# Two transformer blocks on one core: the tiles that TensorE reads are moved to multiples of 512 bytes

## The chip, the cores and the metric

The kernel runs on one NeuronCore of a Trainium2 chip, as one launch. The metric is the device time of an execution in microseconds (us), from which the median of several runs is taken. The engines are named as in the profile: PE is TensorE's matmul, PEld its weight load, DVE is VectorE, ACT is ScalarE, POOL is GpSimd, SP issues DMAs.

## The reference

The input x has 256 tokens of 1,024 features. Two models run one after the other, all in float32:

```python
for i in range(2):                                   # first model, two layers
    x = x + mixer_i(rms_norm(x, norm_mix[i]))        # layer 0: NSA (8 heads) and differential attention (4 heads)
                                                     # layer 1: MoBA attention, 16 heads
    x = x + square(relu(rms_norm(x, norm_mlp[i]) @ mlp_w1[i])) @ mlp_w2[i]      # 1024 -> 4096 -> 1024
x = rms_norm(x, norm_final)
                                                     # second model, one layer
proj = rms_norm(x) @ w_in                            # xa, ga, q, k, v, f, g_a, g_b
y_a = gelu(ga) * rg_lru(conv(xa));  y_b = forgetting_attention(q, k, v, f)
x = x + rms_norm((sigmoid(g_a) * (y_a @ w_proj_a) + sigmoid(g_b) * (y_b @ w_proj_b)) @ w_out)
gate, val = split(conv(rms_norm(x) @ w_up))          # 1024 -> 2 * 3072
x = x + rms_norm((gelu(gate) * val) @ w_down)        # 3072 -> 1024
```

## The kernel before

Activations lie transposed in SBUF, features on the 128 partitions and the 256 tokens along a partition. `x` is the residual stream, 8 feature tiles of 256 tokens. Every projection is computed in the type `float32r` with both operands split in two: a high part and the rest, `a = ah + al`. A product then takes three matmuls: `wh*xh`, `wh*xl`, `wl*xh`.

Weights stream from DRAM. `w_load` fetches a chunk of 1 MB into one of three `raw` buffers by a DMA on SP's queue; `w_parts` splits half a chunk (a unit of 1,024 columns) into `whi` by ACT (L233) and `wlo` by DVE (L234). There are six buffers of 4,096 bytes per partition for each of the two, and `w_next` keeps three units ahead of the one that is used.

Where TensorE multiplies:

- `mm3` (L275, L276, L277): the weights are loaded as the stationary operand, 128 columns, and 256 columns of the activation move through. The activation is `gg_`, the split input of a projection (`gh` and `gl` are its two halves), or `oh` and `ol`, the split output of an attention (tiles `oh`/`ol` of layer 0, `oh1`/`ol1`, `oh2`/`ol2`). `gen_pair` uses it for the projections from the residual stream, `gen_half` for those from an attention.
- `mm2` (L281, L282), in `gen_deep`, for the second matrix of an MLP: 512 columns move in L281 (both halves of `hh`, `hh2` or `yh`), 256 in L282.
- `gen_nat` (L457 to L459) and `gen_wide` (L479 to L481) the other way round: the activation `gg_` is stationary and 256 or 512 columns of `whi` or `wlo` move.

```python
    def mm3(o, wh, wl, xh, xl, start, stop, skip=False):
        nc.tensor.matmul(out=o, lhsT=wh, rhs=xh, start=start, stop=False, skip_group_check=skip)
        nc.tensor.matmul(out=o, lhsT=wh, rhs=xl, start=False, stop=False, skip_group_check=skip)
        nc.tensor.matmul(out=o, lhsT=wl, rhs=xh, start=False, stop=stop, skip_group_check=skip)
```

The order of all work is written out by hand. `weave` interleaves a chain of projection steps with the steps of an attention (`maps_gen`) or of the recurrence (`rg_gen`); elsewhere `run` takes the steps of one projection one after another. The time line of a run: layer 0's projections and attention to 156 us, its MLP to 338, layer 1's attention to 454 and MLP to 636, the second model's mixer to 943, its up projection with convolution and gelu (`evac_up`) to 1085, its down projection to 1157, the end.

Where a tile lies in SBUF follows from the order of the pools and, within a pool, from the order in which its tiles are first asked for; each is rounded up to 32 bytes, and a pool that is closed gives its place to the next. Its place is the same in all 128 partitions. The first bytes in the kernel before, and what is left of them after division by 512:

| tile | first byte | mod 512 |
|---|---|---|
| `vec`, `cs`, `ones` (pool `cp`) | 16512, 18624, 21728 | 128, 192, 224 |
| `x`, `gg_` (pool `xp`) | 22912, 31104 | 384 |
| `acc`, `sq` (pool `np`) | 47488, 51712 | 384, 0 |
| `raw` (three) | 54848 ... | 64 |
| `whi` (six), `wlo` (six) (pool `wp`) | 80192 ..., 104768 ... | 320 |
| `hh` of the first MLP, of the second | 146752, 129344 | 320 |
| `hh2`, `yh` | 129344 | 320 |
| `qT` of layer 0 (pool `a0`) | 146752 | 320 |
| `kcT` of layer 0 | 173824 | 256 |
| `wcmp`, and later in the same place `oh`, `ol` of layer 0 | 176032, 184224 | 416 |
| `oh1`, `ol1`, `oh2`, `ol2` | 155968, 164160, 167232, 175424 | 320 |

Slices of these tiles that TensorE reads begin at multiples of 512 bytes from the tile's first byte, so that a tile's remainder is that of all its reads: `gg_` has 2,048 bytes for a feature tile (1,024 each for the high and the low part), a weight tile 512 bytes for a feature tile and 128 columns.

Of the kernel before, what the change touches and what calls it, by code (L numbers as in the profile page):

```python
# [7 lines left out]
F32 = mybir.dt.float32  # L8
# [61 lines left out]
def kernel(  # L70
# [29 lines left out]
    cp = ctx.enter_context(tc.tile_pool(name="cp", bufs=1))  # L100
    xp = ctx.enter_context(tc.tile_pool(name="xp", bufs=1))
    np_ = ctx.enter_context(tc.tile_pool(name="np", bufs=2))
    rawp = ctx.enter_context(tc.tile_pool(name="rawp", bufs=3))
    wp = ctx.enter_context(tc.tile_pool(name="wp", bufs=6))
    dp = ctx.enter_context(tc.tile_pool(name="dp", bufs=1, space=DRAM))
# [6 lines left out]
    cs = cp.tile([128, NCST], F32, name="cs")  # L112
    ones = cp.tile([128, 128], F32, name="ones")
    mhalf = cp.tile([128, 8], F32, name="mhalf")
    x = xp.tile([128, KT, T], F32, name="x")
    gg_ = xp.tile([128, KT, 2, T], FR, name="gg_")
    g_ = Halves(gg_)
# [4 lines left out]
    def V(n, i=None, m=1):  # L122
        o, w = VEC[n]
        if i is None:
            return vec[:, o:o + w]
        return vec[:, o + i:o + i + m]
# [10 lines left out]
    def add_stream(ap, units, n=None, small=False):  # L137
        for i in range(ap.shape[0] if n is None else n):
            chunks.append((ap[i], units, small))
# [43 lines left out]
    add_stream(w_up, U8)  # L183
    add_stream(w_dn, U8)

    W = Ctl()
    W.raw = []
    W.q = []
    W.ci = 0
    W.ui = 0  # L190
    NT = (7, 11)

    def w_load():
        ci = len(W.raw)
        if ci >= len(chunks):
            return
        ap, units, small = chunks[ci]
        n = sum(a * b for a, b in units)
        if small:
            t = rawp.tile([128, n], F32, tag="raws", name="raws", bufs=1)  # L200
        else:
            t = rawp.tile([128, 2048], F32, tag="raw", name="raw")
        if ci == 0:
            W.part = lambda a, b: nc.sync.dma_start(out=t[:, a:b], in_=ap[:, a:b])
        else:
            nc.sync.dma_start(out=t[:, :n], in_=ap)
        W.raw.append(t)
# [525 lines left out]
    nc.sync.dma_start(out=cs, in_=cst)  # L733
    nc.sync.dma_start(out=vec[:, 72:], in_=vecs[:, 72:])
    w_load()
    tb_t = cp.tile([33, 16], F32, name="tb_t")
    nc.vector.memset(tb_t[32:33, :], NEGB)
    nc.vector.memset(ones, 1.0)
    nc.vector.memset(mhalf, -0.5)
    warm = cp.tile([128, 8], F32, name="warm")  # L740
    nc.scalar.activation(out=warm, in_=mhalf, func=AF.Square)

    wps = pst.tile([128, 512], F32, tag="t", name="wps")
# [78 lines left out]

    A0 = ExitStack()
    ap0 = A0.enter_context(tc.tile_pool(name="a0", bufs=1))
    qT = ap0.tile([128, 4, T], F32, name="qT")
    ksT = ap0.tile([128, T], F32, name="ksT")
    kwT = ap0.tile([128, T], F32, name="kwT")
# [11 lines left out]
    kcT = ap0.tile([128, 2, 16], F32, name="kcT")  # L839
    vcb = ap0.tile([128, 8, 64], F32, name="vcb")  # L840
    nlam = ap0.tile([128, 1], F32, name="nlam")
    wcmp = [ap0.tile([128, 2048], F32, tag="e8", name="wcmp%d" % i, bufs=2) for i in range(2)]
    for i in range(2):
        nc.sync.dma_start(out=wcmp[i], in_=w_cmp[i])

# [289 lines left out]
    nc.vector.tensor_tensor(out=sqs[2], in0=sqs[2], in1=sqs[3], op=ALU.add)  # L1135
    norm.parts = [sqs[k][:, a, :] for k in (0, 2) for a in range(2)]
    norm.tail = 3
    sgain = cp.tile([128, 1], F32, name="sgain")
    have = {}

    def note(n, f):
# [79 lines left out]
    def log1pe(pool, z, n, pre):  # L1221

        e = pool.tile([128, n], F32, name=pre + "e")
        d = pool.tile([128, n], F32, name=pre + "d")
        q = pool.tile([128, n], F32, name=pre + "q")

        def s0():
            nc.vector.scalar_tensor_tensor(out=e, in0=z, scalar=-1.0, in1=z, op0=ALU.mult, op1=ALU.min)
            nc.scalar.activation(out=e, in_=e, func=AF.Exp)

        def s1():
            nc.vector.tensor_scalar(out=d, in0=e, scalar1=2.0, scalar2=None, op0=ALU.add)
            nc.vector.reciprocal(out=d, in_=d)
            nc.vector.tensor_tensor(out=e, in0=e, in1=d, op=ALU.mult)

        def s2():
            nc.vector.tensor_tensor(out=d, in0=e, in1=e, op=ALU.mult)
            nc.vector.tensor_scalar(out=q, in0=d, scalar1=1.0 / 19.0, scalar2=None, op0=ALU.mult)

        def poly(cs_):  # L1240
            for c in cs_:
                nc.vector.scalar_tensor_tensor(out=q, in0=q, scalar=1.0 / c, in1=d, op0=ALU.add, op1=ALU.mult)

        def s7():
            nc.vector.scalar_tensor_tensor(out=q, in0=q, scalar=1.0, in1=e, op0=ALU.add, op1=ALU.mult)
            nc.vector.tensor_scalar(out=q, in0=q, scalar1=2.0, scalar2=None, op0=ALU.mult)

        steps = [s0, s1, s2] + [lambda c=c: poly(c) for c in ((17, 15), (13, 11), (9, 7), (5, 3))] + [s7]
        return steps, q
# [63 lines left out]
        ],  # L1313
        gen_half(0, 4, oh, ol, residual_add, ready=lambda: len(hdone) >= 2),
    )
    nsp = cp.tile([128, 10], F32, name="nsp")
    psp = cp.tile([128, 10], F32, name="psp")
    hb = cp.tile([128, 20], F32, name="hb")
    hm = cp.tile([128, 16], F32, name="hm")
    sp_steps, sp_q = log1pe(cp, V("lam"), 10, "sp")  # L1320

    def sp_fin():
# [15 lines left out]
    bias_ctx.close()  # L1338


    gc = cp.tile([128, 8], F32, name="gc")
    nc.vector.tensor_tensor(out=gc, in0=V("fin"), in1=V("pre2"), op=ALU.mult)
    nA, nB = Norm(), Norm()
    mlp(norm, lambda j: gc[:, j:j + 1], nA, nB)
# [642 lines left out]
```

## Time and profile before

| | |
|---|---|
| median of 3 runs | 1167.9 us (1167.79 to 1168.95) |
| the profiled execution | 1170.1 us, of which 1168.3 us are its span (first to last instruction) |
| granted TensorE clock, mean of the span | 0.987 of full speed |
| PE busy | 1133.2 us, 97% of the span, 8,367 matmuls |
| DVE busy, ACT busy, POOL busy | 69%, 54%, 16% |

A matmul's busy time in the profile overlaps that of the next (a matmul of 256 columns is listed with some 280 ns, and one starts every 113 to 120 ns), so the pace of a stream is read from the starts of its matmuls, and PE's share of busy time only says that it hardly ever stands still.

### The profile page before, as it was taken

To read this page: it belongs to the slowest core of one execution; us is meant where nothing else is said; L and a number is where in the kernel's file an instruction comes from. 1 tells how busy PE (TensorE), PEld (TensorE's weight loads), DVE (VectorE), ACT (ScalarE), POOL (GpSimd) and SP (SyncE) were. 2 spreads that over 40 slices of the span, in tenths; PEclk is the share of its full clock that TensorE was granted. 3 is DMA by queue.
4 is the path that set the end of the run, shared out by engine and by line. 5 is a ranking of instruction groups with operands and counts; after the bars stand their busy time and mean duration, and the time that the engine had idled before them with its cause. 6 is when DMAs were issued, how large, how long until landed. Compare 5 with 4: busy or idle time off the path is not lost.

```text
span 1168.3 us, 20796 instructions
## 1 busy us (share of the span) xinstructions
PE 1133.2 (97%) x8367; PEld 1036.7 (89%) x8367; DVE 806.9 (69%) x1436; ACT 630.7 (54%) x1120; POOL 187.6 (16%) x228
## 2 busy tenths in 40 slices
PE   8999999999999999999999999999999999999996
PEld 7987799998889889999889896899799999999885
DVE  5767766665545776576455787866677589999843
ACT  4446556553434555556444677645464656666642
POOL 2014320000010123000001000032310123222211
PEclk8999999999999999999999999999999989999998
DMA  8841244555454333455455453564455425455641
GB/s 324 291 143 73 74 181 145 201 197 203 158 216 180 116 131 145 151 185 206 188 213 207 152 197 123 173 228 149 158 181 206 175 89 167 163 177 180 208 153 37
DMA packets 31297, 199.90 MB, mean 171 GB/s; under 512 B 3594, under 2 KB 6042, under 8 KB 9056
## 3 DMA queue, kind: packets, MB, share of 16 engines
q1 hardware_dynamic: 28832, 187.23, 44.4%
q0 software_dynamic: 2080, 11.08, 2.9%
q8 instruction: 66, 1.08, 0.4%
q14 instruction: 31, 0.25, 0.1%
q10 hardware_dynamic: 288, 0.26, 0.1%
HBM read 197.43 MB, written 3.22 MB: 172 GB/s over the span
## 4 chain that ended last, share of the span: by engine, by line
PE 77%; DVE 14%; ACT 3%; issue 2%; POOL 2%; DMA 1%; SPq 0%; POOLq 0%; ACTq 0%
PE g L281 15%; PE g L275 14%; PE g L277 13%; PE g L276 13%; PE g L282 7%; DVE y L1693 4%; DVE wlo L234 4%; PE rgp L1462 2%; PE pt L664 1%; PE g L479 1%; PE g L481 1%; PE g L480 1%; PE o L714 1%; ACT whi L233 1%; DVE u L1681 1%
## 5 line engine op out<-in xcount | busy, mean ns | idle before, releaser
L234 DVE TENSOR_TENSOR wlo<-raw,whi 128x1024 fp32r<-128x1024 f32 (+2 forms) x356 | 421.0, 1213 | 107.6 <-ACT whi L233 107.4
L275 PE MATMUL g<-gg__91,whi 128*128 128x256 f32 x1632 | 463.1, 284 | 4.0 <-ACT whi L233 2.4
L277 PE MATMUL g<-gg__91,wlo 128*128 128x256 f32 x1632 | 459.7, 282 | 4.1 <-DVE wlo L234 4.1
L276 PE MATMUL g<-gg__91,whi 128*128 128x256 f32 x1632 | 457.4, 280 | 0.5 <-DVE gg__91 L270 0.4
L233 ACT CAST whi<-raw 128x1024 fp32r<-128x1024 f32 (+2 forms) x356 | 350.2, 1024 | 15.5 <-PE g L276 7.8
L275 PEld LDWEIGHTS g<-gg__91,whi 128*128 128x128 f32 x1632 | 308.5, 189 | 11.5 <-issue 5.4
L277 PEld LDWEIGHTS g<-gg__91,wlo 128*128 128x128 f32 x1632 | 308.4, 189 | 8.3 <-DVE wlo L234 8.2
L276 PEld LDWEIGHTS g<-gg__91,whi 128*128 128x128 f32 x1632 | 308.9, 189 | 1.2 <-DVE gg__91 L270 0.7
L281 PE MATMUL g<-hh,whi 128*128 128x512 f32 x704 | 247.4, 397 | 1.4 <-DVE u L1681 1.4
L282 PE MATMUL g<-hh,wlo 128*128 128x256 f32 x704 | 196.8, 280 | 0.2 <-DVE wlo L234 0.2
L281 PEld LDWEIGHTS g<-hh,whi 128*128 128x128 f32 x704 | 132.2, 188 | 33.6 <-ACT q L1702 1.7
L282 PEld LDWEIGHTS g<-hh,wlo 128*128 128x128 f32 x704 | 132.6, 188 | 0.5 <-DVE wlo L234 0.5
L339 POOL TENSOR_TENSOR acc<-acc,sq 128x256 f32<-128x256 f32 x53 | 42.3, 805 | 463.8 <-ACT sq L335 462.8
L653 POOL TENSOR_TENSOR p<-p,rr 128x384 f32<-128x384 f32 x56 | 49.1, 877 | 210.6 <-DVE rr L648 80.1
L638 ACT ACTIVATE p<-p,nm 128x256 f32<-128x256 f32 x112 | 49.9, 449 | 45.2 <-DVE nm L629 45.0
L1693 DVE SCALAR_TENSOR_TENSOR y<-u,cw,y 128x255 f32<-128x255 f32 (+1 forms) x96 | 60.2, 687 | 0.0
L275 PE MATMUL g<-oh,whi 128*128 128x256 f32 x192 | 55.6, 290 | 0.0
L277 PE MATMUL g<-oh,wlo 128*128 128x256 f32 x192 | 54.3, 283 | 0.0
L1208 ACT ACTIVATE u<-u 128x512 f32<-128x512 f32 x32 | 20.2, 632 | 62.8 <-DVE u L1207 62.8
L276 PE MATMUL g<-ol,whi 128*128 128x256 f32 x192 | 54.1, 282 | 0.0
L750 DVE TENSOR_TENSOR x<-x,g 128x256 f32<-128x256 f32 x32 | 13.5, 421 | 56.7 <-PE g L282 56.2
L267 DVE TENSOR_TENSOR hh<-u,hh 128x512 fp32r<-128x512 f32 x32 | 22.2, 693 | 43.2 <-ACT hh L266 43.2
(325 smaller groups left out, 1340.7 us busy)
## 6 DMA issues: line engine op xcount, KB each, us to landing
raw<-in_w_in_dram SPq DMA_DIRECT2D x30, 1024.0 KB, 4.9
raw<-in_w_up_dram SPq DMA_DIRECT2D x24, 1024.0 KB, 4.9
raw<-in_w_m1a_dram SPq DMA_DIRECT2D x16, 1024.0 KB, 4.8
raw<-in_w_m2a_dram SPq DMA_DIRECT2D x16, 1024.0 KB, 4.9
raw<-in_w_m1b_dram SPq DMA_DIRECT2D x16, 1024.0 KB, 4.8
raw<-in_w_m2b_dram SPq DMA_DIRECT2D x16, 1024.0 KB, 4.9
raw<-in_w_od_dram SPq DMA_DIRECT2D x12, 1024.0 KB, 4.9
raw<-in_w_dn_dram SPq DMA_DIRECT2D x12, 1024.0 KB, 4.8
```

Of the source, the lines that this page charges most:

```text
L233: nc.scalar.copy(out=hi[:, a:b], in_=t[:, off + a:off + b])
L234: nc.vector.tensor_tensor(out=lo[:, a:b], in0=t[:, off + a:off + b], in1=hi[:, a:b].bitcast(F32), op=ALU.subtract)
L275: nc.tensor.matmul(out=o, lhsT=wh, rhs=xh, start=start, stop=False, skip_group_check=skip)
L276: nc.tensor.matmul(out=o, lhsT=wh, rhs=xl, start=False, stop=False, skip_group_check=skip)
L277: nc.tensor.matmul(out=o, lhsT=wl, rhs=xh, start=False, stop=stop, skip_group_check=skip)
L281: nc.tensor.matmul(out=ps.rearrange("p a t -> p (a t)"), lhsT=wh, rhs=X.both(k), start=start, stop=False, skip_group_check=True)
L282: nc.tensor.matmul(out=ps[:, 0, :], lhsT=wl, rhs=X.h[:, k, :], start=False, stop=stop, skip_group_check=True)
L339: nc.gpsimd.tensor_tensor(out=self.acc, in0=self.acc, in1=dst, op=ALU.add)
L638: nc.scalar.activation(out=p[:, c0:c1], in_=p[:, c0:c1], func=AF.Exp, scale=-1.0, bias=nm[:, b:b + 1], accum_out=sm[:, b:b + 1],)
L653: nc.gpsimd.tensor_tensor(out=pv, in0=pv, in1=w, op=ALU.mult)
L1462: nc.tensor.matmul(out=ps[c, m, :], lhsT=w[:, m, prs[pi], c], rhs=xc[:, half * 5 + pi, :], start=n == 0, stop=n == len(nb), skip_group_che ...
L1693: nc.vector.scalar_tensor_tensor(out=y[:, a, d:], in0=u[:, a, 0:T - d], scalar=cw[:, w, c:c + 1], in1=y[:, a, d:], op0=ALU.mult, op1=ALU.add)
```

## The change

No instruction is added, removed or reordered. Two tiles that nothing writes or reads (`pad`) are put in, of 128 bytes per partition ahead of `x` and of 64 ahead of the weight buffers; the small tiles of pool `cp` are asked for at its start; and in layer 0's pool `wcmp` is asked for first and no longer after `nlam`.

```diff
+    def pad(pool, n):
+        pool.tile([128, n], F32, tag="pad", name="pad", bufs=1)
+
     rawp = ctx.enter_context(tc.tile_pool(name="rawp", bufs=3))
     wp = ctx.enter_context(tc.tile_pool(name="wp", bufs=6))
...
     mhalf = cp.tile([128, 8], F32, name="mhalf")
+    tb_t = cp.tile([33, 16], F32, name="tb_t")
+    warm = cp.tile([128, 8], F32, name="warm")
...
+    gc = cp.tile([128, 8], F32, name="gc")
+    pad(xp, 32)
     x = xp.tile([128, KT, T], F32, name="x")
     gg_ = xp.tile([128, KT, 2, T], FR, name="gg_")
...
+    pad(wp, 16)
     W = Ctl()
...
     ap0 = A0.enter_context(tc.tile_pool(name="a0", bufs=1))
+    wcmp = [ap0.tile([128, 2048], F32, tag="e8", name="wcmp%d" % i, bufs=2) for i in range(2)]
     qT = ap0.tile([128, 4, T], F32, name="qT")
...
     nlam = ap0.tile([128, 1], F32, name="nlam")
-    wcmp = [ap0.tile([128, 2048], F32, tag="e8", name="wcmp%d" % i, bufs=2) for i in range(2)]
```

## Rows read from the trace of the kernel before

**Rows 1.** The page's first lines: span; busy time, share and instructions by engine.
```profile
span 1168.3 us, 20796 instructions
PE 1133.2 (97%) x8367; PEld 1036.7 (89%) x8367; DVE 806.9 (69%) x1436; ACT 630.7 (54%) x1120; POOL 187.6 (16%) x228
```

**Rows 2.** The chain of work that ended last, shares by engine.
```profile
PE 77%; DVE 14%; ACT 3%; issue 2%; POOL 2%; DMA 1%; SPq 0%; POOLq 0%; ACTq 0%
```

**Rows 3.** Stretches: length, busy PE, PEld, DVE, ACT, POOL; clock; DMA share; GB/s.
```profile
184.00:248.00 64.00, 64.00 (x546) 64.00 (x545) 44.34 (x49) 37.84 (x48) 0.00 (x0) 1.00 0.56 198
649.00:710.00 61.00, 61.00 (x461) 50.97 (x462) 54.66 (x102) 42.49 (x72) 0.90 (x4) 1.00 0.41 151
943.00:1085.00 142.00, 138.25 (x1138) 134.59 (x1137) 137.91 (x211) 96.48 (x162) 39.74 (x47) 1.00 0.48 163
```

**Rows 4.** PE's waits, of the list the one for split weights: us, times, longest.
```profile
PE g L277 <- DVE wlo L234: 4.1, 19, 0.4
```

**Rows 5.** The costliest groups of the page: busy us, mean ns; idle before.
```profile
L234 DVE TENSOR_TENSOR wlo<-raw,whi 128x1024 fp32r<-128x1024 f32 (+2 forms) x356 | 421.0, 1213 | 107.6 <-ACT whi L233 107.4
L275 PE MATMUL g<-gg__91,whi 128*128 128x256 f32 x1632 | 463.1, 284 | 4.0 <-ACT whi L233 2.4
L281 PE MATMUL g<-hh,whi 128*128 128x512 f32 x704 | 247.4, 397 | 1.4 <-DVE u L1681 1.4
```

**Rows 6.** Timeline of PE, start and length: two streams on `gg_`, first and last.
```profile
183.61 0.28 PE L275 MATMUL g<-gg__91,whi 128*128 128x256 f32 x1
...
247.91 0.28 PE L275 MATMUL g<-gg__91,whi 128*128 128x256 f32 x1
...
679.44 0.28 PE L276 MATMUL g<-gg__91,whi 128*128 128x256 f32 x1
...
702.22 0.28 PE L276 MATMUL g<-gg__91,whi 128*128 128x256 f32 x1
```

**Rows 7.** Timeline of PE: two streams on attention outputs, first matmul and next stream's first.
```profile
145.49 0.29 PE L275 MATMUL g<-oh,whi 128*128 128x256 f32 x1
...
156.29 0.28 PE L275 MATMUL g<-gg__91,whi 128*128 128x256 f32 x1
...
885.27 0.28 PE L275 MATMUL g<-oh,whi 128*128 128x256 f32 x1
...
908.30 0.28 PE L275 MATMUL g<-gg__91,whi 128*128 128x256 f32 x1
```

**Rows 8.** Timeline of PE: second matrix of the first MLP, then of the second.
```profile
248.27 0.39 PE L281 MATMUL g<-hh,whi 128*128 128x512 f32 x1
...
338.01 0.40 PE L281 MATMUL g<-hh,whi 128*128 128x512 f32 x1
...
546.89 0.39 PE L281 MATMUL g<-hh,whi 128*128 128x512 f32 x1
...
635.64 0.28 PE L275 MATMUL g<-gg__91,whi 128*128 128x256 f32 x1
```

**Rows 9.** Timeline of PE: part of a stream with moving weights.
```profile
71.31 0.28 PE L459 MATMUL g<-whi,gg__91 128*128 128x256 f32 x1
...
73.70 0.28 PE L459 MATMUL g<-whi,gg__91 128*128 128x256 f32 x1
```

**Rows 10.** Timeline of PE: sums of squares, one moving column, 128 stationary ones.
```profile
19.07 1.05 PE L346 MATMUL nsum<-ones,qT 128*128 128x1 f32 x8
19.98 1.03 PE L346 MATMUL nsum<-ones,kvd 128*128 128x1 f32 x8
20.88 0.28 PE L275 MATMUL gs<-gg__91,whi 128*24 128x256 f32 x1
...
932.06 1.05 PE L346 MATMUL nsum<-ones,sq 128*128 128x1 f32 x8 [0.53 <-ACT sq L335]
```

**Rows 11.** Timeline of PE: a projection to 16 columns, so 16 stationary columns.
```profile
711.07 0.28 PE L276 MATMUL gs<-gg__91,whi 128*16 128x256 f32 x1
...
712.66 0.39 PE L479 MATMUL g<-whi,gg__91 128*128 128x512 f32 x1
```

More of the change, by code (lines that the diff above doesn't have):

```diff
@@ L114 @@
     mhalf = cp.tile([128, 8], F32, name="mhalf")
+    tb_t = cp.tile([33, 16], F32, name="tb_t")
+    warm = cp.tile([128, 8], F32, name="warm")
+    sgain = cp.tile([128, 1], F32, name="sgain")
+    nsp = cp.tile([128, 10], F32, name="nsp")
+    psp = cp.tile([128, 10], F32, name="psp")
+    hb = cp.tile([128, 20], F32, name="hb")
+    hm = cp.tile([128, 16], F32, name="hm")
+    gc = cp.tile([128, 8], F32, name="gc")
+    pad(xp, 32)
     x = xp.tile([128, KT, T], F32, name="x")
@@ L735 @@
     w_load()
-    tb_t = cp.tile([33, 16], F32, name="tb_t")
     nc.vector.memset(tb_t[32:33, :], NEGB)
@@ L739 @@
     nc.vector.memset(mhalf, -0.5)
-    warm = cp.tile([128, 8], F32, name="warm")
     nc.scalar.activation(out=warm, in_=mhalf, func=AF.Square)
@@ L1137 @@
     norm.tail = 3
-    sgain = cp.tile([128, 1], F32, name="sgain")
     have = {}
@@ L1315 @@
     )
[L1316 to L1319, printed above, removed]
     sp_steps, sp_q = log1pe(cp, V("lam"), 10, "sp")
@@ L1338 @@
     bias_ctx.close()
-    gc = cp.tile([128, 8], F32, name="gc")
     nc.vector.tensor_tensor(out=gc, in0=V("fin"), in1=V("pre2"), op=ALU.mult)
```

## The prediction

> **What bounds the kernel now.** I read the page's engine table first: PE is busy 97% of the span, and no other engine over 69% [rows 1]. The chain of waits says the same from the other side: 77% of the chain that ended last is PE work, 14% DVE [rows 2]. Next the stretches. In a plain projection, 184 to 248 us, PE fills all of its time while DVE works 44 of 64 us; from 943 to 1085 us, the up projection, DVE works 137.9 of 142 us, so there PE follows DVE and a faster PE wins nothing [rows 3]. PE's waits are short: the late half of the split weights costs 4.1 us in 19 waits over the whole run [rows 4]. So outside the up projection the time is the number of matmuls times the pace at which PE starts them.
>
> That pace is the place to look, because a change of addresses can act on nothing else. The groups give 284 ns for a matmul of 256 columns [rows 5], but they overlap; the timeline gives starts. On `gg_` from 183.61 to 247.91 us there are 546 steps: 117.8 ns each. From 679.44 to 702.22 us, same line, same tiles, 201 steps: 113.3 ns [rows 6]. On `oh` of layer 0 90 steps take 10.80 us, on `oh2` 192 steps take 23.03 us: 120.0 ns in both [rows 7]. In the second matrix of the first MLP 254 pairs (L281 and L282, 512 and 256 columns) take 89.74 us, 353.3 ns a pair; in the second MLP 256 pairs take 88.75 us, 346.7 ns [rows 8]. The clock was at full speed, 2.4 GHz (granted 1.00), in all the stretches of [rows 3], and if a column takes a cycle, which I assume, 256 are 106.7 ns, so 6.6 to 13.3 ns of every matmul are stall.
>
> Two things are to be seen. First, identical tiles run at two paces: a stream keeps one of them for a long time and can change it only after an interruption. That is a phase between PE's two SBUF reads, the moving operand of one matmul and the weights of the next. Second, the worst pace belongs to addresses. Moving tile and weights lie at (384, 320) mod 512 for `gg_`: 117.8 or 113.3. They lie at (320, 320) for `oh2` and (416, 320) for layer 0's `oh`: 120.0. With the roles exchanged, weights moving at 320 and `gg_` stationary at 384, 21 steps take 2.39 us, 113.8 ns [rows 9].
>
> **The change part by part.** The tiles of `cp` that are asked for earlier were already in `cp`; their sum is unchanged and `x` would still begin at 22912 = 44 x 512 + 384. The pad of 128 bytes takes it and `gg_` to 0. Everything behind moves by 128, `whi` and `wlo` to 448, and the pad of 64 takes these to 0. From there all pools lie 192 bytes further, and 320 + 192 = 512: `hh`, `hh2`, `yh`, `oh1`, `ol1`, `oh2`, `ol2` reach 0. Layer 0's `oh` and `ol` take the place of `wcmp`, now first in its pool: 0. So all pairs become (0, 0), which no row of before has.
>
> The instructions are the same in the same order on every engine and queue; SP and POOL issue the same DMAs. The pads are never written. One reuse moves: with `wcmp` first, the early part of the first MLP's `hh` lies where `oh` and `ol` were. Their last reader ends before 156.6 us, and PE has left them for `gg_` at 156.29 [rows 7]; nothing can be written to `hh` before the MLP's own first products, later on the same engine. No wait, cost 0.
>
> What remains is the pace at (0, 0). The bounds from the rows: if only one of the two reads is at work, alignment shows nothing. Weight loads alone (one moving column) take 1.05 us for eight at 320 and 1.05 us for eight at 0, and the eight from 19.98 to 20.88 us are 112 ns apart [rows 10]. Moving reads nearly alone, with weights of 16 columns, at 384: 14 steps in 1.59 us, 113.6 ns [rows 11]. So the stall above 113 ns is a conflict of the two reads. 320 is an odd multiple of 64, 384 is a multiple of 128. Count the operands off 128: none has been seen; one gives 117.8 or 113.3, whichever side it is on; two give 120.0, for 416 as for 320, though their distances differ (96 and 0). [...] With none off, I take the better pace that the trace shows for the same work.
>
> The sum, outside the first 25 us and the up projection, over gaps that no wait interrupts, by the timeline's starts:
> - L275 to L277 on `gg_`: of 4,896, some 3,720 (1,127 in the up projection and 48 in the start win nothing), mean 117.0 ns over 3,611 steps (676 are already at 113.3). To 113.3: 3.65 x 3,611 = 13.1 us.
> - the same on the attention outputs: 555 steps at a mean of 119.8, 6.5 ns each: 3.6 us.
> - second MLP matrices and `yh`: about 770 pairs at a mean of 350.9 to 346.7: 3.2 us. Two thirds are at 353.3 now, a third at 346.7 [rows 8].
> - `gen_nat` and `gen_wide`: 135 and 186 steps, 0.7 us together.
>
> In all 20.6 us. Against the profiled execution that is 1170.1 - 20.6 = 1149.5; this execution lies 2.2 us above the median of the runs, so the median goes from 1167.9 to 1147.3. The cover: ACT and DVE must split weights some 3% faster. A unit of 24 matmuls lasts 24 x 113.3 = 2.72 us, a split of `wlo` 1.21 us [rows 5], and in the stretch at 113.3 ns, where the recurrence runs too, DVE was at 54.7 of 61 us and PE still full [rows 3]. If DVE falls behind there, nothing is lost, since that stretch is at the target already. Bounds: below, all pairs down to the weight loads' 112 ns, about 34 us by the same counts (5.0 x 3,611, 7.8 x 555, and 12.3 x 770 with a pair at 2 x 113.3 + 112 = 338.6, 1.7 for the rest); above, 120.0 everywhere (next part).
>
> **The rivals.**
> - *Equal remainders collide more.* The trace's only pairs with the same remainder in all their steps are (320, 320), and `oh2` is never at anything but 120.0 once settled [rows 7]. After the change all pairs are equal. If distance decides and not the multiple of 128, `gg_` goes from 117.0 to 120.0: 3.0 x 3,611 = 11.0 us, 0.7 for the small streams: 1167.9 + 11.7 = 1179.6. It decides as soon as the mean on `gg_` is over 117.0 plus what the other tiles give. Against: (416, 320) is as bad at another distance, and `hh` at (320, 320) does have a better state [rows 8].
> - *Addresses decide nothing, phase does.* The Trainium skill, page "SBUF — State Buffer", section "Who interferes with whom", gives PE two independent read ports and says that it waits on no one; alignment would then win nothing, 1167.9. Apart from the page: if a stream keeps the phase of its last restart and restarts fall as before, it is 1167.9. If all streams fell into the slow one, 676 steps x 4.45 and 256 pairs x 6.6 would be lost, 4.7 us, and 1.1 us won where 120.0 falls to 117.8: 1171.5. Against it stand 120.0 on two sets of attention tiles and 117.8 or 113.3 on `gg_` with the same loop [rows 6, 7].
> - *Aligned reads are better than anything seen.* Weight loads set the pace: 1167.9 - 34 = about 1134.
>
> **How the numbers follow.** Forecast, alignment frees the stalls to the better pace or part of the way to it (1140 to 1158): 0.45. Beyond that, down to the loads' pace: 0.10. Addresses decide nothing, or gains and losses cancel: 0.15, most of it within 0.2%, which is 2.3 us and about what a measurement of this kernel can tell from no change. Equal remainders collide, or the slow phase wins: 0.30, 1171 to 1181. I predict 1147.3. A range from 1136 to 1180 leaves out some 0.05 at the lower end and 0.1 at the upper; the forecast's own range is 1140 to 1158. Faster 0.55, same 0.13, slower 0.32.
>
> **What would show it.** Right: the timeline on `gg_` outside the up projection at 113.3 ns or less from start to start in nearly all streams, `oh` and `oh2` as fast as `gg_`, the first MLP's pairs at 346.7 or less, granted clock, weight split and DMA rows unchanged, and the up projection still 142 us long. Wrong: 120.0 on `gg_` (the first rival), the same mixture of 113.3 and 117.8 with `oh` still apart (the second), or PE at a better pace but waiting for `wlo` by as much as it wins, which would move the bound to DVE.

## The result: slower by 0.9%

| | before | after |
|---|---|---|
| median of three runs | 1167.9 us | 1179.0 us (1177.84 to 1179.56) |
| ratio to before, 95% interval | | 1.0091, 1.0068 to 1.0114 |
| profiled execution, its span | 1170.1 us, 1168.3 us | 1177.84 us, 1176.1 us |
| mean pace of L288 to L290 on `gg_`, outside the up projection | 117.0 ns | 119.9 ns |

I had predicted 1147.3 us and faster; the range, to 1180, holds the result, but at the end of the first rival, "equal remainders collide more", which gave 1179.6.

The changed kernel's lines stand 13 further down than before in the helpers, so L275 to L277 are now L288 to L290, L281 and L282 are L294 and L295, L233 and L234 are L246 and L247. First the page's opening lines and the chain's shares by engine, which answer to [rows 1, 2]:

```profile
span 1176.1 us, 20795 instructions
PE 1144.4 (97%) x8367; PEld 1049.9 (89%) x8367; DVE 808.6 (69%) x1436; ACT 630.1 (54%) x1120; POOL 187.7 (16%) x228
PE 78%; DVE 14%; ACT 3%; issue 2%; POOL 2%; DMA 1%; SPq 0%; POOLq 0%; ACTq 0%; DVEq 0%
```

PE is busy 11.2 us longer with the same 8,367 matmuls; DVE, ACT and POOL are within 1.7 us of before. Nothing was added and nothing waits more: PE itself is slower. The costliest groups say how (busy us, mean ns of one, then idle time before them and what ended most of it):

```profile
L247 DVE TENSOR_TENSOR wlo<-raw,whi 128x1024 fp32r<-128x1024 f32 (+2 forms) x356 | 421.6, 1214 | 107.0 <-ACT whi L246 106.8
L288 PE MATMUL g<-gg__100,whi 128*128 128x256 f32 x1632 | 469.6, 288 | 4.0 <-ACT whi L246 2.5
L290 PE MATMUL g<-gg__100,wlo 128*128 128x256 f32 x1632 | 465.6, 285 | 1.4 <-DVE wlo L247 0.2
L294 PE MATMUL g<-hh,whi 128*128 128x512 f32 x704 | 248.0, 398 | 1.4 <-DVE u L1686 1.4
```

L288's mean rises from 284 to 288 ns [rows 5], while the split of the weights keeps its 1.21 us and PE's wait for `wlo` falls from 4.1 us [rows 4] to 0.2. The stretches of [rows 3], same columns:

```profile
184.00:248.00 64.00, 64.00 (x536) 64.00 (x535) 43.35 (x49) 37.12 (x48) 0.00 (x0) 1.00 0.56 198
943.00:1085.00 142.00, 138.03 (x1094) 134.30 (x1095) 136.27 (x214) 94.73 (x163) 39.87 (x48) 0.98 0.45 155
```

In the plain projection, with the clock at full speed in both, 536 matmuls fit where 546 did. The second stretch now takes in the head of the up projection, whose first matmul starts at 946.20 us where it started at 937.28: up to 951.4 us PE's granted clock is 0.50 there (1.2 GHz), as it was up to 943.7 before, hence the 0.98. By the starts of its matmuls the up projection lasts 147.4 us before and 147.5 now. The timeline of PE gives the pace (start, length):

```profile
183.72 0.28 PE L288 MATMUL g<-gg__100,whi 128*128 128x256 f32 x1
...
250.32 0.40 PE L294 MATMUL g<-hh,whi 128*128 128x512 f32 x1
...
340.77 0.40 PE L492 MATMUL g<-whi,gg__100 128*128 128x512 f32 x1
...
550.50 0.40 PE L294 MATMUL g<-hh,whi 128*128 128x512 f32 x1
...
640.95 0.28 PE L288 MATMUL g<-gg__100,whi 128*128 128x256 f32 x1
...
689.80 0.28 PE L288 MATMUL g<-gg__100,whi 128*128 128x256 f32 x1
...
710.20 0.28 PE L290 MATMUL g<-gg__100,wlo 128*128 128x256 f32 x1
...
894.28 0.28 PE L288 MATMUL g<-oh,whi 128*128 128x256 f32 x1
...
917.32 0.28 PE L288 MATMUL g<-gg__100,whi 128*128 128x256 f32 x1
```

From 183.72 to 250.32 us there are 555 steps: 120.0 ns each, where [rows 6] had 117.8. From 689.80 to 710.20 there are 170: again 120.0, where [rows 6] had 113.3 in the same projection. No stream on `gg_` keeps a faster pace. `oh2`, 192 steps from 894.28 to 917.32, is at 120.0 as in [rows 7]. The second matrices of the two MLPs (256 pairs from 250.32, 256 from 550.50) are at 353.3 ns a pair each; in [rows 8] the second had 346.7.

The balance, by starts: 3,611 x 2.9 = 10.5 us more on `gg_`; the second MLP 256 x 6.7 = 1.7 more; `gen_nat`, now at 120.0, 0.6 more; the 186 wide steps fell from 233.2 to 228.2, 0.9 less; the last projection's pairs (`hh2`) fell from 353.4 to 346.7 in their long stretch, some 1.0 less. Together 10.9. The medians differ by 11.1, the two profiled executions by 7.8 only: the one of the kernel before lies 2.2 us above its median, that of the changed kernel 1.2 below. By the starts, these 3 us lie in the first 25 us and in steps that a wait or another operation interrupts.

### The profile page after: what moved, and what is told of

Read it like the earlier page. It is cut to its first block, busy times and chain, and to the rows that moved or that the text cites. A ratio compares the mean times of both kernels' runs of the same rounds, so it can differ in the third digit from the quotient of the medians.

```text
span 1176.1 us, 20795 instructions
## 1 busy us (share of the span) xinstructions
PE 1144.4 (97%) x8367; PEld 1049.9 (89%) x8367; DVE 808.6 (69%) x1436; ACT 630.1 (54%) x1120; POOL 187.7 (16%) x228
## 4 chain that ended last, share of the span: by engine, by line
PE 78%; DVE 14%; ACT 3%; issue 2%; POOL 2%; DMA 1%; SPq 0%; POOLq 0%; ACTq 0%; DVEq 0%
PE g L294 15%; PE g L288 14%; PE g L289 14%; PE g L290 14%; PE g L295 7%; DVE y L1698 4%; DVE wlo L247 4%; PE rgp L1467 2%; PE pt L677 1%; PE g L492 1%; PE o L727 1%; PE g L494 1%; PE g L493 1%; DVE u L1686 1%; PE s L633 1%
## 5 line engine op out<-in xcount | busy, mean ns | idle before, releaser
L247 DVE TENSOR_TENSOR wlo<-raw,whi 128x1024 fp32r<-128x1024 f32 (+2 forms) x356 | 421.6, 1214 | 107.0 <-ACT whi L246 106.8
L288 PE MATMUL g<-gg__100,whi 128*128 128x256 f32 x1632 | 469.6, 288 | 4.0 <-ACT whi L246 2.5
L290 PE MATMUL g<-gg__100,wlo 128*128 128x256 f32 x1632 | 465.6, 285 | 1.4 <-DVE wlo L247 0.2
L289 PE MATMUL g<-gg__100,whi 128*128 128x256 f32 x1632 | 464.1, 284 | 0.5 <-DVE gg__100 L283 0.4
L246 ACT CAST whi<-raw 128x1024 fp32r<-128x1024 f32 (+2 forms) x356 | 349.7, 1022 | 16.2 <-PE g L289 7.9
L288 PEld LDWEIGHTS g<-gg__100,whi 128*128 128x128 f32 x1632 | 315.0, 193 | 11.4 <-issue 5.5
L290 PEld LDWEIGHTS g<-gg__100,wlo 128*128 128x128 f32 x1632 | 314.8, 193 | 5.1 <-DVE wlo L247 5.1
L289 PEld LDWEIGHTS g<-gg__100,whi 128*128 128x128 f32 x1632 | 315.0, 193 | 1.2 <-DVE gg__100 L283 0.7
L294 PE MATMUL g<-hh,whi 128*128 128x512 f32 x704 | 248.0, 398 | 1.4 <-DVE u L1686 1.4
L295 PE MATMUL g<-hh,wlo 128*128 128x256 f32 x704 | 197.2, 280 | 0.1
L294 PEld LDWEIGHTS g<-hh,whi 128*128 128x128 f32 x704 | 132.2, 188 | 33.8 <-ACT q L1707 1.7
L295 PEld LDWEIGHTS g<-hh,wlo 128*128 128x128 f32 x704 | 132.8, 189 | 0.4 <-DVE wlo L247 0.4
L288 PE MATMUL g<-oh,whi 128*128 128x256 f32 x192 | 55.6, 290 | 0.0
L290 PE MATMUL g<-oh,wlo 128*128 128x256 f32 x192 | 54.3, 283 | 0.0
```

The source lines that it names most:

```text
L246: nc.scalar.copy(out=hi[:, a:b], in_=t[:, off + a:off + b])
L247: nc.vector.tensor_tensor(out=lo[:, a:b], in0=t[:, off + a:off + b], in1=hi[:, a:b].bitcast(F32), op=ALU.subtract)
L294: nc.tensor.matmul(out=ps.rearrange("p a t -> p (a t)"), lhsT=wh, rhs=X.both(k), start=start, stop=False, skip_group_check=True)
L295: nc.tensor.matmul(out=ps[:, 0, :], lhsT=wl, rhs=X.h[:, k, :], start=False, stop=stop, skip_group_check=True)
```

## The experiments

Two theories stood after the result. *Distance*: what counts is how far the first byte of the moving tile and that of the stationary tile lie from each other modulo some power of two, and distance 0 is bad. *Place*: what counts is where each of them lies against a boundary, and the multiple of 512 itself is bad. The expectations name a third, *restart*: any shift deals the two paces anew.

### The streams by themselves

A program with nothing but matmuls on tiles begun at chosen bytes. "Pair" below is the three-product stream of L288 to L290 (ns a matmul), "deep" the pairs of L294 and L295 (ns for both), "wide" 512 moving columns. Each was begun three times, after interruptions of different length.

```
CASES = [(d, 0) for d in (0, 16, 32, 48, 64, 80, 96, 112, 128, 192, 256, 384)] + [
    (64, 64), (32, 32), (0, 64), (0, 32), (0, 96)]   # (moving, stationary)
```

> Not the two blocks: matmul streams alone, on two tiles whose places are chosen (moving at m, weights at w bytes past a multiple of 512), each pair with the loops of mm3, of mm2 and with 512 moving columns, restarted three times; the output is not the blocks' one. If the distance of the two reads decides, and with a period of 128 bytes: at (0,0), (128,0), (256,0), (384,0), (64,64) and (32,32) the mm3 stream runs at 120.0 ns a matmul; at (64,0), (192,0) and (0,64) at 117.8 or 113.3, by the restart. If the place of each tile by itself decides: (64,64) and (32,32) differ from (0,0), and (128,0) from (256,0). If neither, all pairs show the same mixture. For 16, 32, 48, 80, 96, 112 no theory has a number; one below 113.3 would be the place to put the tiles.

Measured, first byte of the moving and of the stationary tile past a multiple of 512:

| moving, stationary | pair | deep | wide |
|---|---|---|---|
| 0, 0 | 120.0 119.9 119.9 | 346.4 346.4 353.0 | 226.6 to 228.6 |
| 64, 64 | 119.8 120.0 119.9 | 353.5 | 227.7 |
| 32, 32 | 119.8 | 346.6 346.6 353.9 | 227 |
| 256, 0 | as 0, 0 | as 0, 0 | as 0, 0 |
| 32, 0 | 117.7 | 346.7 to 347.0 | 233.2 |
| 64, 0 | 117.8 117.8 117.8 | 353.5 | 229 |
| 0, 64 | 113.3 117.8 117.8 | 352.7 | 233.4 |
| 96, 0 | 120.0 | 350.4 to 353.2 | 234 |
| 112, 0 | 113.8 113.8 113.8 | 353.3 | 231 |
| 128, 0 and 384, 0 | 118.6 118.5 120.0 | 351 | 232.5 |
| 192, 0 | 113.3 117.8 113.3 | 353 | 233.4 |

The pairs left out (16, 48, 80 to 0, and 0 to 32, 96) took 116.6 to 120.1 in the three-product stream.

The timeline of this program's PE: fifth and last matmul of the first stream at (0, 0), then of the first at (112, 0):

```profile
15.97 0.28 PE L58 MATMUL p0w0x<-ma,wa 128*128 128x256 f32 x1
...
21.13 0.28 PE L59 MATMUL p0w0x<-ma,wa 128*128 128x256 f32 x1
...
359.31 0.28 PE L58 MATMUL p112w0x<-ma,wa 128*128 128x256 f32 x1
...
364.20 0.28 PE L59 MATMUL p112w0x<-ma,wa 128*128 128x256 f32 x1
```

Between these stand 43 steps: 5.16 us or 120.0 ns, and 4.89 us or 113.7 ns. With no other engine at work, equal remainders give 120.0 wherever they lie, and 256 apart is as 0. The pace of (0, 0) is the streams' own, not the kernel's. What I had not looked for: 112 takes 113.8 at every restart, where 192 depends on the restart, and 64 has 117.8 here and both paces in the kernel before [rows 6].

### The same in the kernel: take one pad, or move both tiles

Without the pad ahead of the weights, `gg_` stays at 0 and everything behind it lies at 448, 64 away, as before the change:

```diff
-    pad(wp, 16)
```

> The changed kernel without the 64 bytes ahead of the weight buffers: gg_ at 0, weights and all later tiles at 448, so gg_ and weights are 64 bytes apart and the attention outputs and hh at the weights' own remainder. Distance theory: gg_ back to 117.8 or 113.3 ns, mean some 117; oh at 120.0; 1168 us, within 3 of the kernel before. Place theory (tiles at a multiple of 512 are slow): gg_ stays at 0 and stays near 120.0: 1177 to 1180. Restart theory (any shift deals the phases anew): anywhere from 1160 to 1180, with both paces on gg_.

Without the pad ahead of `x`, all tiles lie at 384, equal but on no multiple of 512:

```diff
-    pad(xp, 32)
```

> The changed kernel without the 128 bytes ahead of x: gg_, weights and all later tiles at 384, equal remainders, none at a multiple of 512. Distance theory: 120.0 ns on gg_ and on the attention outputs, 1179 us like the changed kernel. Place theory (a multiple of 512 is what slows): gg_ at 384 is where it was before, so 117.8 or 113.3 and 1166 to 1170. Restart theory: both paces on gg_.

`gg_` and all tiles behind the weights 64 past them, so that `oh`, `oh1`, `oh2` are no longer equal to the weights either:

```diff
+    zp = ctx.enter_context(tc.tile_pool(name="zp", bufs=1))
+    pad(zp, 16)
...
-    pad(xp, 32)
+    pad(xp, 48)
...
-    pad(wp, 16)
```

> Weights at 0, gg_ and all later tiles at 64: every pair of a projection is 64 bytes apart, the attention outputs and hh too. Distance theory: 117.8 or 113.3 ns on gg_ and now also on oh, oh1, oh2 (576 matmuls, 2.2 to 6.5 ns each, 1 to 4 us); 1163 to 1168 us. Place theory (a tile off a multiple of 512 stalls, one at it does not): nothing to tell it from the kernel before but the weights, 1160 to 1175. Restart theory: both paces, any mixture, 1160 to 1180.

| | median, us | ratio to before, 95% | `gg_` pace outside the up projection | `oh2` pace | pairs of the two MLPs |
|---|---|---|---|---|---|
| `gg_` at 0, weights 448 | 1168.82 | 0.9992, 0.9981 to 1.0003 | 117.1 | 120.0 | 346.6 |
| all at 384 | 1178.57 | 1.0076, 1.0060 to 1.0091 | 119.9 | 120.0 | 353.3 |
| 64 apart throughout | 1170.77 | 1.0014, 1.0000 to 1.0028 | 117.7 | 117.8 | 353.3, 348.9 |

In the first of these, the stream that fills the stretch of [rows 6]:

```profile
183.37 0.28 PE L287 MATMUL g<-gg__100,whi 128*128 128x256 f32 x1
...
247.68 0.39 PE L293 MATMUL g<-hh,whi 128*128 128x512 f32 x1
```

546 steps, 117.8 ns each: with `gg_` at 0 as in the change, but the weights 64 away, the pace of before is back and with it the time. All at 384 is as slow as all at 0. Place has fallen, and restart with it, for all at 384 is a shift too and shows 119.9, no mixture; the loss is the equality. The third kernel won what distance says on `oh2` (120.0 to 117.8) but no time: the expected 1 to 4 us went to streams on `gg_` that nearly all fell into the slower of their two paces (117.7 in the mean outside the up projection, not 117.0) and to the MLP pairs, 353.3 in the first MLP and 348.9 in the second. For pairs the table has 64 apart as a bad place, 353.5 at all restarts; for `gg_` the restart decides between two paces, so a gain of that size can be lost by luck.

### Finer distances, and a shorter weight load

```
CASES = [(d, 0) for d in (8, 24, 104, 108, 116, 120, 124, 136, 144, 160, 176, 208, 224, 240, 368)] + [
    (176, 64), (64, 176), (0, 144), (240, 128)]
NARROW = [(0, 0), (64, 0), (112, 0), (128, 0)]   # 16 stationary columns in place of 128
```

> Leaves the two blocks out, as the first of these programs did: only streams of matmuls, with the moving tile and the stationary tile begun at chosen bytes, three restarts of each. New distances (moving first byte minus stationary first byte): 8, 24, 104 to 144, 160, 176, 208, 224, 240, 368 bytes; and 112 from other bases (176 and 64; 240 and 128) and 112 the other way round (0 and 144; 64 and 176). Four streams have weights of 16 columns in place of 128. Theory D (the time of one matmul is set by the distance of the two reads modulo 256 bytes): 368, (176,64), (240,128) and (0,144) repeat the 113.8 ns that (112,0) took; (64,176) does as (144,0) does. Theory B (112 was good because of where that tile lay): (176,64) and (240,128) take 117 to 120 ns. On whether it is the weight load that is disturbed or the moving read itself: if the two reads meet in the same part of the memory and the load, which is near its limit of 112 ns, is what runs late, a stream with 16-column weights takes about 113.6 ns at every distance; if the moving read is itself held up however short the load, it takes about 120 ns at (0,0) too. If 112 lies in a narrow valley, its neighbours 104, 108, 116 and 120 show 117 to 120; if a broad one, 113 to 115.

| moving, stationary | pair | deep | wide |
|---|---|---|---|
| 108, 0 | 120.0 | 346.6 | 230 |
| 116, 0 | 121.7 121.7 121.7 | 356.4 | 240.0 |
| 368, 0 | 113.7 113.8 113.8 | 353.3 | 231 |
| 176, 64 | 114.3 113.6 113.8 | 353.3 | 226.7 |
| 240, 128 | 114.2 113.3 113.3 | 353.3 | 231 |
| 0, 144 | 118.4 120.0 119.8 | 349.4 | 226.7 to 233.5 |
| 144, 0 | 118.7 | 346.4 | 233.4 |
| 64, 176 | 120.0 | 353.3 | 233.3 |
| 16 columns, all four distances | 113.3 to 113.4 | | |

The distances left out took 117.1 to 120.1, but for one restart of (120, 0) at 122.3.

Timeline of this program: fifth and last matmul at (116, 0); two weight loads, not next to each other, of the stream of 512 columns at (116, 0); then fifth and last matmul with 16 stationary columns at (0, 0):

```profile
213.07 0.29 PE L59 MATMUL p116w0x<-ma,wa 128*128 128x256 f32 x1
...
218.30 0.29 PE L60 MATMUL p116w0x<-ma,wa 128*128 128x256 f32 x1
...
259.87 0.19 PEld L76 LDWEIGHTS p116w0x<-ma,wa 128*128 128x128 f32 x1
...
260.35 0.19 PEld L76 LDWEIGHTS p116w0x<-ma,wa 128*128 128x128 f32 x1
...
949.89 0.28 PE L100 MATMUL p0n0x<-ma,wa 128*16 128x256 f32 x1
...
954.76 0.28 PE L101 MATMUL p0n0x<-ma,wa 128*16 128x256 f32 x1
```

43 steps each of 256 columns: 121.6 and 113.3 ns. With a load of 16 columns none of the four distances makes a difference: so the long load is needed for the stall. That the load is what runs late, at 128 columns near its limit of 112 ns [rows 10], is not shown. The streams of 512 columns speak against it: the two loads shown are two steps of 240 ns apart and last 0.19 us each, so a load has time to spare in every step, and still the step is 240.0 ns at (116, 0) and 226.7 at (176, 64). There the moving read seems to be what is held up while a load goes on. For 256 columns, with both reads near their limits, the runs do not tell which of them is late.

112 apart is good with the weights at 0, 64 and 128, and 256 further on, but four bytes to either side of it lie 120.0 and 121.7: a narrow valley. And distance is not the whole: (0, 144) is 112 apart modulo 256 as well and took 118.4 to 120.0. The weights begin there at an odd multiple of 16; where they did so in (64, 176), the pace was no better than (144, 0)'s either. Why, stays open.

### Only `gg_` moved, to 112 bytes

The allocator places tiles in steps of 32 bytes, so `gg_` becomes a slice of a larger tile; the pads are set so that weights and all else keep equal remainders modulo 256.

```diff
-    pad(xp, 32)
...
-    gg_ = xp.tile([128, KT, 2, T], FR, name="gg_")
+    gg_t = xp.tile([128, 4096 + 64], FR, name="gg_")
+    gg_ = gg_t[:, 60:4156].rearrange("p (k a t) -> p k a t", a=2, t=T)
...
-    pad(wp, 16)
+    pad(wp, 48)
```

> The changed kernel with gg_ alone moved so that it begins 112 bytes past a multiple of 256 while weights and all other tiles keep equal remainders. Theory D (distance): the 3,611 matmuls of the three-product streams go from 119.9 to 113.8 ns, 22.0 us less; the 186 wide ones go from 228.2 to about 231 (0.5 us more); oh, oh1, oh2, hh, hh2 stay as in the changed kernel. About 1157 us, which is faster than both kernels. Rival 1 (in the whole kernel other reads and writes of the memory keep the streams at the mixture of before, 117.0): 3,611 x 2.9 = 10.5 us less, about 1168. Rival 2 (the pace is now set by something else once PE is faster, the split of the weights by ScalarE and VectorE): PE's paces are 113.8 where it runs without a break, but waits appear between streams and the time stays above 1163.

1161.09 us, ratio to before 0.994 (0.9926 to 0.9953): 17.9 us less than the changed kernel, of the 21.5 that distance gave. The timeline of the long stream, and of the costliest groups the two with waits:

```profile
182.99 0.28 PE L288 MATMUL g<-gg__99,whi 128*128 128x256 f32 x1
...
245.25 0.39 PE L294 MATMUL g<-hh,whi 128*128 128x512 f32 x1
```

```profile
L288 PE MATMUL g<-gg__99,whi 128*128 128x256 f32 x1632 | 459.4, 282 | 4.5 <-ACT whi L246 3.0
L290 PE MATMUL g<-gg__99,wlo 128*128 128x256 f32 x1632 | 455.5, 279 | 7.0 <-DVE wlo L247 7.0
```

549 steps at 113.4 ns; most streams of 22 steps between two interruptions take 114.8 to 115.8, and the mean is 114.1. Over the whole kernel outside the up projection, the unbroken steps on `gg_` take 20.8 us less than in the changed kernel; 2.1 us come back in the steps that a wait or another operation interrupts, and 0.9 in the wide ones, now at 233.3. The wait for `wlo` rose to 7.0 us, but 6.4 of these lie between 928 and 1076 us, in the up projection that DVE bounds. So the second rival of that run, the split as the new bound, is right only there, where it was expected from the start.

### Four bytes further, and the other tiles

First, against the kernel with `gg_` at 112:

```diff
-    gg_ = gg_t[:, 60:4156].rearrange("p (k a t) -> p k a t", a=2, t=T)
+    gg_ = gg_t[:, 61:4157].rearrange("p (k a t) -> p k a t", a=2, t=T)
```

> The kernel with gg_ 112 bytes apart, with gg_ alone moved by 4 more bytes, to 116. If the distance decides and the streams alone are the right measure, its three-product streams take the 121.7 ns that (116,0) took alone: against the changed kernel 3,611 x (121.7 - 119.9) = 6.5 us more, the wide ones 186 x (240 - 228.2) = 2.2 us more, together about 1187 us, the slowest of all, though no remainder is shared. Rival (any unequal remainders are better than equal ones): below the 1179 of the changed kernel.

1186.67 us, ratio to before 1.0157 (1.0143 to 1.0171), `gg_` at 121.7 ns. Four bytes from the best placement of `gg_` lies the slowest kernel of all, 25.6 us away, and no remainder is equal there between `gg_` and the weights.

The attention outputs to 112 bytes, by slices of larger tiles, again against the kernel with `gg_` at 112:

```diff
+    def off(pool, name, **kw):
+        t = pool.tile([128, KT * T + 64], FR, name=name, **kw)
+        return t[:, 28:28 + KT * T].rearrange("p (k t) -> p k t", t=T)
...
-    oh = fp.tile([128, KT, T], FR, name="oh2")
+    oh = off(fp, "oh2")
```

(and the same for `ol2`, `oh1`, `ol1` and layer 0's `oh` and `ol`, with `wcmp` widened to the same size).

> The kernel with gg_ 112 bytes apart, with oh, ol, oh1, ol1, oh2, ol2 moved to 112 as well. Distance theory: their 555 matmuls counted in unbroken streams (576 in all) go from 119.8 to 113.8 ns, 3.3 to 3.5 us less: 1161.1 to about 1157.7 us. Rival (those streams are held up by something else, since they took 120.0 in both the kernel before and the changed one, at equal remainders in each): 1161.

1159.55 us, ratio to before 0.9926 (0.9913 to 0.994). `oh2` runs at 113.3 ns, `oh` at 115.5, `oh1` at 115.1. By these paces 182 x 4.2 + 181 x 4.8 + 192 x 6.6 = 2.9 us were won; the profiled executions of this kernel and that with `gg_` alone at 112 differ by 2.2, the medians by 1.5, less than half of the 3.3 to 3.5 expected. Stretches of `oh` and `oh1` of ten steps stay at 116.6 to 118.7 ns; those of 94 and 106 steps reach 113.7 and 113.8.

Last, `hh`, `yh` and `hh2` 32 bytes from the weights, by a tile of 32 bytes ahead of each, and one of 224 behind `yh` (here `hh`, against the kernel just shown):

```diff
+        hp.tile([128, 8], F32, name="pada")
         H = Halves(hp.tile([128, 32, 2, T], FR, name="hh"))
```

> The kernel with gg_ and the oh tiles at 112, with hh, yh and hh2 moved to 32 bytes from the weights. Streams alone took 346.7 to 347.0 ns a pair there, with no restart at 353. Distance theory: the 512 pairs of the two MLPs go from 353.3 to 346.7, 3.4 us less; hh2 stays at 346.4: about 1154.3 us. Rival (the pairs of the two MLPs are at 353.3 for another reason than their place): no change to the kernel before it in this list, about 1157.7.

1155.04 us, ratio to before 0.9889 (0.9875 to 0.9902). The timeline of the first MLP's second matrix, then of `oh2`:

```profile
245.31 0.39 PE L298 MATMUL g<-hh,whi 128*128 128x512 f32 x1
...
334.05 0.39 PE L496 MATMUL g<-whi,gg__99 128*128 128x512 f32 x1
...
873.77 0.28 PE L292 MATMUL g<-oh,whi 128*128 128x256 f32 x1
...
895.53 0.28 PE L292 MATMUL g<-gg__99,whi 128*128 128x256 f32 x1
```

256 pairs in 88.74 us are 346.6 ns a pair, 192 steps in 21.76 us are 113.3 ns. Both kernels are beaten, the one before by 1.1%, by addresses alone.

## Why the prediction was wrong

**The bound: right.** Outside the up projection the time is the count of matmuls times the pace of their starts. The balance of the result closes with paces alone (10.9 of the 11.1 us between the medians), and the up projection kept its length, 147.4 and 147.5 us. Waits and the first 25 us moved by no more than the 3 us by which the two profiled executions stray from their medians.

**The mechanism: right as far as it is shown.** I read the stall above 113 ns as a conflict of PE's two reads, from weight loads that do not care where they lie [rows 10] and narrow weights that leave the moving read at 113.6 [rows 11]. The streams with 16 stationary columns bear it out: 113.3 to 113.4 at all four distances. Which of the two reads is held up stays open. The Trainium skill has this otherwise: page "SBUF — State Buffer", section "Who interferes with whom", calls the two read ports of PE independent. Here the measurement decides: 113.3, 117.8, 120.0 and 121.7 ns for the same matmul by the distance and, at some distances, the restart.

**The step that failed: the count of operands off 128.** From three placements I ordered the paces by how many operands lie off a multiple of 128, and read (0, 0) as the best. The rows allowed distance as well; I set it aside because (416, 320) and (320, 320) were both at 120.0 at different distances, 96 and 0. The streams alone show that both are bad by themselves: (96, 0) takes 120.0 and so does (0, 0). They show too that the count orders nothing: with none off 128, 120.0 at (0, 0) and 118.5 to 120.0 at (128, 0); with one off, 113.8 at (112, 0) and 121.7 at (116, 0); with two off, 113.6 to 114.3 at (176, 64). Two bad distances out of two looked like evidence that distance does not matter. The only three-product streams with equal remainders that the trace had were at 120.0, all of them; that was the nearest row to (0, 0), and I passed it for a rule made up to fit three points.

**The choice of pace: wrong with it.** I took 113.3 for the value that no row had, the best seen. The row of equal remainders [rows 7] gives 120.0: 3.0 x 3,611 on `gg_` and 0.7 for the small streams, 1179.6, the first rival, at 0.30 with its neighbours. It measured 119.9 and 1179.0. Its parts were not all as written: the wide steps got faster by 5.0 ns, and the pairs of the second MLP slower.

**What else the prediction said.** That ACT and DVE can split faster: shown by the kernel with `gg_` 112 apart, whose wait for `wlo` rose only where DVE already was the bound. That every stream could be brought to the better pace, 20.6 us in all: in part, and by other addresses. `gg_` at 112 has a mean of 114.1 ns, 2.9 x 3,611 = 10.5 of the 13.1 us counted for it, and the time fell by 7.0 us against the kernel before; with the other tiles moved it is 13.2. The stall was counted from an assumed 106.7 ns for 256 columns; no placement tried went below 113.3, not even with 16 stationary columns.

## What to carry to other kernels

When a stream of matmuls with a weight load each runs slower than its moving columns alone, compare the start addresses of moving and stationary tile with each other, not with a boundary: aligning both to the same boundary gave 120.0 ns, 112 bytes apart 113.8, and 116 apart 121.7. Measure the stream alone at several distances first; in this case such a table foretold the last four kernels to within 4.1 us, with `gg_` and the attention outputs at 112 short of their forecasts in short streams. And when a rule is made from three rows, look for the row that is nearest to the new case before trusting the rule.

## What was not expected of the hardware

- The pace of a 128-column load with 256 moving columns of four bytes each depends on the distance of the two tiles with a period of 256 bytes (256 as 0, 384 as 128, 368 as 112), in steps as fine as 4 bytes: 108, 112, 116 gave 120.0, 113.8, 121.7 ns. With the weights at 144 or 176 it did not hold: 118.4 to 120.0 at (0, 144), 120.0 at (64, 176).
- Distances differ by stream. 0 is among the worst for the three-product stream (120.0) and among the best for 512 columns (227; 240.0 at 116); 112 is best for the three-product stream and no help to the pairs of 512 and 256 columns (353.3), which took 346.4 to 347 at 32, 108 or 144.
- At some distances a stream has two paces and keeps the one it starts with: 113.3 or 117.8 at (192, 0) and (0, 64), 346.4 or 353.0 for pairs at (0, 0). At (112, 0) and (116, 0) all three restarts of the three-product stream agree. What sets the pace at a restart was not tried.
- The distance counted only at the full clock. In the head of the up projection, at a granted clock of 0.50 (1.2 GHz) after some 6 us in which PE ran twelve short matmuls, the stream on `gg_` takes 213.3 ns a step at all four distances looked at: 64 (the kernel before), 0 (the changed one), 112 and 116. That is 256 columns at one a cycle. Of the kernel with 116, which is the slowest at the full clock, 18 steps:

```profile
955.55 0.41 PE L288 MATMUL g<-gg__99,whi 128*128 128x256 f32 x1
...
959.39 0.41 PE L288 MATMUL g<-gg__99,whi 128*128 128x256 f32 x1
```
